# Stick-breaking attention: the sums over later keys from two fp32r parts of the softplus instead of one fp32 tile

## The chip, the cores and the metric

The kernel runs on one core of one Trainium2 chip. The metric is the device time of one execution in microseconds (us), as a median over runs. The profile is of one execution.

## The reference, cut to what matters

The program is a conditioned block (a convolution module and a feed-forward block) and then two blocks with feed-forward layers, one with an RWKV mixer and one with stick-breaking attention, on 256 positions of width 1024. Only the stick-breaking attention is touched: 12 heads of 64, computed for each pair of heads on its own.

```python
z = einsum('bhtd,bhsd->bhts', q, k) * scale
before = s_pos < t_pos
log_keep = where(before, -softplus(z), 0.0)
later = cumsum(log_keep, axis=3, reverse=True) - log_keep
att = where(before, exp(log_sigmoid(z) + later), 0.0)
out = einsum('bhts,bhsd->bhtd', att, v)
```

`later` is a sum over all keys after s. As log_sigmoid(z) = z - softplus(z), the exponent is z minus a sum of softplus over the keys from s on, and a matrix product with a triangle of -1 gives that sum.

## The kernel before, in words

All weights stream through SBUF. Each 128x1024 piece is split by `Stream` into a high fp32r part (ScalarE, L226) and a low one (VectorE, L235), and each product of the large layers is three fp32r matmuls of 256 columns (L377, L378, L372, and L448, L450, L452 for the values). The activations are split in the same way by `split_act` (L625 on ScalarE, L626 on VectorE). Small products of the mixers are plain fp32 matmuls: the profile shows two records for each of them, "x2" where it shows one for an fp32r matmul.

In `StickBreaking`, keys lie on partitions and queries on columns. A head has a z tile of 384 columns in PSUM: 256 queries for the first 128 keys, and 128 queries for the last 128. For a pair p of heads `attention` goes through these steps:

- `scores`: two fp32 matmuls for each head into z (L2294, L2295), then Abs and Exp on ScalarE into e (L2298, L2299);
- `log_keep`: Ln on ScalarE (L2305), max and add on VectorE (L2306), which makes the softplus in e, and the triangular mask on GpSimd (L2308);
- `attend`: three fp32 matmuls for each head add minus the sums to z (L2316 with 256 columns, L2317 and L2319 with 128), then VectorE (L2320) and Exp on ScalarE (L2322);
- `values`: e times V (L2332, L2334), a copy (L2336) and later `split_act` by `operand`.

The steps of pair p - 1 lie between those of pair p: scores p, attend p - 1, log_keep p, values p - 1.

The order of all instructions is written out by `weave`, a planner that runs when the program is built; each engine then works strictly in that order. `weave` has a clock `now` in planned us of TensorE and a clock `dve` of VectorE (it starts at 12.0), and a list of tasks: the attention (priority 1), two tasks of the attention to the memory (3), the projections as `main` (5), and after `main` has ended `products` (5), the first products with the output weights. Each step of a task yields its cost on TensorE, on VectorE, and a further delay. The next task that is due takes a step, by priority; after a step with TensorE cost of another task, `main` comes first. Where no task is due, `idle` writes dummy matmuls of 256 columns (L1455) until one is:

```python
                    self.now += pe
                    t[1] = self.now + more
                    turn = pe > 0 and t[2] is not main
                    if dve:
                        self.dve = max(self.dve, self.now + 0.2) + dve
                        if t[2] is not main:
                            t[1] = self.dve + more + 0.1
...
                later = [t[1] for t in self.tasks if t[1] > self.now]
                self.idle(min(later) - self.now)
                self.now = min(later)
...
        n = int(us / 0.11)
```

`t[1]` is when the task is due again. The costs of `main` are 1.42 for each of the first eight steps, 2.6 (VectorE 1.1) for half a block of values, and 0.66 for each quarter of a projection (VectorE 1.1 at the first quarter of the four). A memory task takes the steps (0.86, 0.7, 0), (0, 0, 1.5), (0, 0.7, 0.3), (0.86, 0, 2.0), (0.86, 0, 1.0) twice. `products` costs 0.66 a step, 16 steps in all, and starts when both memory tasks are done and `n_att` is 5 (`while len(self.mem_out) < 2 or self.n_att < NP - 1: yield`), that is when attend 4 has been issued; its four accumulators take the PSUM banks of the attention. The rest of the output product, the layer norm and the last feed-forward block follow.

At the start `project` fetches the constants of this stage (`sbc`, by a DMA on ScalarE's queue, L2184), loads a table (L342), fills `negones` on GpSimd (L2188), and copies two queries (L2196); the first projections follow.

Of the kernel before, what the change touches and what calls it, by code (L numbers as in the profile page):

```python
# [8 lines left out]
F32 = mybir.dt.float32  # L9
F32R = mybir.dt.float32r  # L10
AF = mybir.ActivationFunctionType
# [4 lines left out]
P = 128  # L16
# [1302 lines left out]
class Norm:  # L1319
# [13 lines left out]
    def sum(self, k0, k1, eng):  # L1333

        b, q = self.b, self.q
        for k in range(k0, k1):
            t = b.ys[:, k]
            self.n += 1
            if eng is None or self.n > KD - self.late:
                self.rest.append(t)  # L1340
            elif eng not in self.sums:
                self.sums[eng] = (t, None)
            else:
                prev, out = self.sums[eng]
                if out is None:
                    out = b.tmp.tile([P, 2, T], F32, name="nsum", tag=f"nsum{len(self.sums)}", bufs=1)
                e = b.nc.vector if eng == "dve" else b.nc.gpsimd
                e.tensor_tensor(out=out[:, q:2, :], in0=prev[:, q:2, :], in1=t[:, q:2, :], op=ALU.add)  # L1348
                self.sums[eng] = (out, out)
# [805 lines left out]
class StickBreaking(Mixer):  # L2155
# [25 lines left out]
    def project(self):  # L2181
        nc, b, mp = self.nc, self.b, self.mp
        sbc = mp.tile([P, 640], F32, name="sbc")
        nc.scalar.dma_start(out=sbc, in_=b.dr["consts_sb"])  # L2184
        b.exp_and_log()
        self.sbk = {n: sbc[:, COFF[n][0]:sum(COFF[n])] for n, _ in CONSTS_SB}
        self.negones = mp.tile([P, P], F32, name="negones")
        nc.gpsimd.memset(self.negones, -1.0)  # L2188
        ys = b.ys.rearrange("p k a t -> p (k a) t")
        self.V = ys[:, 0:6].rearrange("p (a f) t -> p a (f t)", a=2)  # L2190
        self.os = ys[:, 6:12]
        self.mq = ys[:, 14:16]
        self.qk, self.n_val = {}, 0
        pre, b.pre = b.pre, None
        for i in range(2):
            nc.scalar.copy(out=self.mq[:, i, :], in_=pre[2 + i])  # L2196
        self.qk[0] = pre[:2]
        self.add(self.attention(), 1)
        for tl in range(2):
            self.add(self.mem_attention(tl, ys[:, 12 + tl]), SB_MEM)  # L2200
        early = [b.gu_tile() for _ in range(2)]
        yield from b.gemm_outs_parts(early, b.xx)
        for n in range(2):
            self.queries(n + 1, [early[n][:, i, :] for i in range(2)])
        self.mem_go = True
        for kind, i in SB_ORDER[2:]:
            if kind == "p":
                yield from self.pair(i)
                continue
            gu = b.gu_tile()  # L2210
            for u in range(2):
                list(b.gemm_tok(gu, b.xx, u))
                if u:
                    nc.scalar.copy(out=self.V[:, :, i * T:i * T + T], in_=gu)
                    self.n_val += 1
                yield 2.6, 1.1, 0.0
# [41 lines left out]
    def attention(self):  # L2258

        yield 0.0, 0.0, 7.0  # L2260
        self.n_att = 0
        prev = None
        for p in range(NP + 1):
            cur = None
            if p < NP:
                wait = p not in self.qk
                while p not in self.qk:
                    yield
                if wait:
                    yield 0.0, 0.0, 1.0  # L2270
                cur = [self.scores(h, *self.qk[p]) for h in range(2)]
                yield 1.3, 0.9, 0.0
            if prev:
                for z, e in prev:
                    self.attend(z, e)
                self.n_att = p
                yield 1.7, 0.9, 0.0
            if cur:
                for z, e in cur:
                    self.log_keep(z, e)  # L2280
                yield 0.0, 0.9, 0.0
            if prev:
                while self.n_val <= (p - 1) // 2:
                    yield
                yield from self.values(p - 1, prev)
            prev = cur
# [21 lines left out]
        nc.gpsimd.tensor_tensor(out=d, in0=d,  # L2308
                                in1=self.sbk["tri"].unsqueeze(1).to_broadcast([P, 2, P]), op=ALU.mult)

    def attend(self, z, e):

        nc = self.nc
        mm = nc.tensor.matmul
        nt = self.sbk["negtri"]
        mm(z[:, 0:256], lhsT=nt, rhs=e[:, 0:256], start=False, stop=True, skip_group_check=True)  # L2316
        mm(z[:, 128:256], lhsT=self.negones, rhs=e[:, 256:384], start=False, stop=True,  # L2317
           skip_group_check=True)
        mm(z[:, 256:384], lhsT=nt, rhs=e[:, 256:384], start=False, stop=True, skip_group_check=True)  # L2319
        nc.vector.scalar_tensor_tensor(out=e, in0=z, scalar=0.0, in1=self.sbk["bias"], op0=ALU.min,  # L2320
                                       op1=ALU.add)
        nc.scalar.activation(out=e, in_=e, func=AF.Exp)  # L2322
# [38 lines left out]
```

## Time and profile before

| what | value |
|---|---|
| median of 3 runs | 1480.18 us (1478.29 to 1483.04) |
| the profiled execution's own time | 1478.92 us |
| its span, first to last instruction | 1477.1 us |
| granted TensorE clock, mean | 0.976 |
| busy: TensorE, VectorE, ScalarE, GpSimd | 96%, 73%, 58%, 8% |

The projections and the attention of this stage lie from about 1162 to 1262 us of the span. A row of the timeline gives start and duration in us, engine, line, operation, operands and a count; a matmul's duration holds its way through the array, so that the pace of a run of matmuls is read from their starts, not from their durations.

### The profile page before, as it was taken

Reading aid. Unit: us, or ns where it says so; the run is one execution under the profiler, and the core shown is the slowest. Engines: PE = TensorE matmul, PEld = TensorE weight load, DVE = VectorE, ACT = ScalarE, POOL = GpSimd, SP = SyncE. Lnnn points to the kernel's source line nnn. Section 1 sums busy time; section 2 is a strip of 40 time slices with the busy share of each in tenths; the row PEclk is TensorE's granted clock in tenths of the full one; section 3 lists DMA queues with packets and bytes.
Section 4 is the critical chain, followed back from the end, with each engine's and each line's share of the span. In section 5 each row is a group of like instructions: output and inputs, shape, how many; then the busy total and the mean of one; then the engine's idle time right before and its main releaser. Section 6 shows DMA issues by size and latency. Waiting matters only on the chain. (4 is left out here: it accounts for less than half of the span.)

```text
span 1477.1 us, 26067 instructions
## 1 busy us (share of the span) xinstructions
PE 1412.8 (96%) x10664; PEld 1268.2 (86%) x10664; DVE 1074.2 (73%) x1698; ACT 853.8 (58%) x1509; POOL 120.2 (8%) x113
## 2 busy tenths in 40 slices
PE   8888899999999999998999999999999999999997
PEld 7868799998788888898798888888888888888886
DVE  8897788885777667897578776687766755787754
ACT  7686566685656535751346555466554666566542
POOL 1210100001000010040010000110001111100011
PEclk9998899999999999998999999999999999999998
DMA  9775445566355554330034555436545332265540
GB/s 377 295 232 191 178 145 198 200 222 218 124 201 191 200 187 149 109 121 3 2 114 171 200 179 192 184 133 226 195 176 199 126 141 86 95 225 194 198 174 29
DMA packets 39145, 250.38 MB, mean 170 GB/s; under 512 B 4337, under 2 KB 4849, under 8 KB 12274
## 3 DMA queue, kind: packets, MB, share of 16 engines
q1 hardware_dynamic: 38594, 247.60, 46.4%
q8 instruction: 84, 1.38, 0.4%
q10 hardware_dynamic: 432, 1.11, 0.2%
q14 instruction: 35, 0.29, 0.1%
HBM read 247.65 MB, written 1.05 MB: 168 GB/s over the span
## 5 line engine op out<-in xcount | busy, mean ns | idle before, releaser
L235 DVE TENSOR_TENSOR wlo<-wraw,whi 128x1024 fp32r<-128x1024 f32 x416 | 514.4, 1250 | 33.8 <-ACT whi L226 33.2
L226 ACT CAST whi<-wraw 128x1024 fp32r<-128x1024 f32 x416 | 426.4, 1045 | 23.8 <-PE acc L378 6.4
L384 PE MATMUL acc<-hx,whi 128*128 128x512 f32 x880 | 310.8, 398 | 0.0
L384 PE MATMUL acc<-xx,whi 128*128 128x512 f32 x816 | 284.1, 390 | 0.0
L372 PE MATMUL gu<-xx,wlo 128*128 128x256 f32 x1008 | 278.3, 281 | 2.8 <-ACT xx L625 1.7
L372 PE MATMUL acc<-xx,wlo 128*128 128x256 f32 x1008 | 279.4, 282 | 0.0
L372 PE MATMUL acc<-hx,wlo 128*128 128x256 f32 x880 | 247.5, 281 | 0.0
L384 PEld LDWEIGHTS acc<-hx,whi 128*128 128x128 f32 x880 | 165.4, 188 | 40.6
L372 PEld LDWEIGHTS gu<-xx,wlo 128*128 128x128 f32 x1008 | 188.6, 188 | 7.0 <-ACT xx L625 2.9
L372 PEld LDWEIGHTS acc<-xx,wlo 128*128 128x128 f32 x1008 | 189.6, 190 | 0.8
L384 PEld LDWEIGHTS acc<-xx,whi 128*128 128x128 f32 x816 | 153.2, 188 | 32.1
L372 PEld LDWEIGHTS acc<-hx,wlo 128*128 128x128 f32 x880 | 166.1, 189 | 0.0
L384 PE MATMUL gu<-xx,whi 128*128 128x512 f32 x432 | 150.9, 390 | 0.0
L377 PE MATMUL gu<-xx,whi 128*128 128x256 f32 x512 | 148.0, 289 | 2.3 <-ACT u L894 2.3
L378 PE MATMUL gu<-xx,whi 128*128 128x256 f32 x512 | 143.1, 279 | 0.0
L1331 ACT ACTIVATE ys<-ys 128x256 f32<-128x256 f32 (+1 forms) x66 | 28.6, 436 | 152.2 <-DVE ys L1249 135.2
L377 PEld LDWEIGHTS gu<-xx,whi 128*128 128x128 f32 x512 | 96.2, 188 | 9.2 <-issue 6.4
L378 PEld LDWEIGHTS gu<-xx,whi 128*128 128x128 f32 x512 | 96.3, 188 | 0.7 <-issue 0.7
L384 PEld LDWEIGHTS gu<-xx,whi 128*128 128x128 f32 x432 | 81.1, 188 | 17.0
L1348 POOL TENSOR_TENSOR nsum<-ys 128x512 f32<-128x512 f32 (+1 forms) x9 | 12.5, 1386 | 900.0 <-PE acc L384 451.8
L858 ACT COPY lows<-acc 128x256 f32<-128x256 f32 x55 | 20.6, 374 | 97.8 <-PE acc L384 97.7
L1247 DVE SCALAR_TENSOR_TENSOR ys<-xr,acc 128x256 f32<-128x256 f32 x32 | 13.5, 422 | 74.8 <-PE acc L384 74.8
(412 smaller groups left out, 2342.0 us busy)
## 6 DMA issues: line engine op xcount, KB each, us to landing
wraw<-in_w SPq DMA_DIRECT2D x208, 1024.0 KB, 4.8
mraw<-in_mod SPq DMA_DIRECT2D x48, 512.0 KB, 5.8
xr<-in_x SPq DMA_DIRECT2D x2, 512.0 KB, 4.3
m<-in_mem SPq DMA_DIRECT2D x1, 1024.0 KB, 8.2
out<-xr SPq DMA_DIRECT2D x3, 256.0 KB, 2.2
cst<-in_consts SPq DMA_DIRECT2D x1, 546.0 KB
lora<-in_lora ACTq DMA_DIRECT2D x1, 384.0 KB, 3.2
lora_g<-in_lora ACTq DMA_DIRECT2D x1, 384.0 KB, 3.8
```

The costliest lines, as they stand in the source:

```text
L226: b.nc.scalar.copy(out=hi, in_=raw)
L235: b.nc.vector.tensor_tensor(out=lo, in0=raw, in1=hi.bitcast(F32), op=ALU.subtract)
L372: self.nc.tensor.matmul(out, lhsT=wl, rhs=x[:, 0, :], start=start, stop=False, skip_group_check=True)
L377: mm(out, lhsT=wh, rhs=x[:, 0, :], start=start, stop=False, skip_group_check=True)
L378: mm(out, lhsT=wh, rhs=x[:, 1, :], start=False, stop=False, skip_group_check=True)
L384: self.nc.tensor.matmul(bank, lhsT=wh, rhs=x, start=False, stop=stop, skip_group_check=True)
L858: nc.scalar.copy(out=lows[:, 1, :], in_=banks[1][:, 1, :])
L1247: self.nc.vector.scalar_tensor_tensor(out=y, in0=self.xr[:, k, :], scalar=2 * ALPHA, in1=ps[:, 1, :], op0=ALU.mult, op1=ALU.add)
L1331: b.nc.scalar.activation(out=b.ys[:, k0:k1, 1, :], in_=y, func=AF.Square)
L1348: e.tensor_tensor(out=out[:, q:2, :], in0=prev[:, q:2, :], in1=t[:, q:2, :], op=ALU.add)
```

## The change

The softplus tile e is no longer the moving operand. `e_parts` splits it into a high and a low fp32r part (`split_act`: a ScalarE copy and a VectorE subtraction of 128x384, for each head), and `attend` runs each of its three products once for each part, as an fp32r matmul. The two stationary matrices (the triangle and all -1) are held as fp32r in `negs`, made on ScalarE from `sbc` at the start of the stage; the memset on GpSimd goes away. The yields of the attention change with it.

```diff
-        self.negones = mp.tile([P, P], F32, name="negones")
-        nc.gpsimd.memset(self.negones, -1.0)
+        self.negs = mp.tile([P, 2, P], F32R, name="negs")
+        nc.scalar.copy(out=self.negs[:, 0, :], in_=self.sbk["negtri"])
+        nc.scalar.activation(out=self.negs[:, 1, :], in_=self.sbk["negtri"], func=AF.Copy, scale=0.0,
+                             bias=-1.0)
...
             if prev:
-                for z, e in prev:
-                    self.attend(z, e)
+                parts = [self.e_parts(e) for _, e in prev]
+                yield 0.0, 1.1, 0.0
+                for (z, e), x in zip(prev, parts):
+                    self.attend(z, e, x)
                 self.n_att = p
-                yield 1.7, 0.9, 0.0
+                yield 0.9, 0.9, 0.0
...
+    def e_parts(self, e):
+        x = self.mp.tile([P, 2, 384], F32R, name="ep", bufs=2)
+        self.b.split_act(x[:, 0, :], x[:, 1, :], e)
+        return x
+
-    def attend(self, z, e):
+    def attend(self, z, e, x):
...
-        nt = self.sbk["negtri"]
-        mm(z[:, 0:256], lhsT=nt, rhs=e[:, 0:256], start=False, stop=True, skip_group_check=True)
-        mm(z[:, 128:256], lhsT=self.negones, rhs=e[:, 256:384], start=False, stop=True,
-           skip_group_check=True)
-        mm(z[:, 256:384], lhsT=nt, rhs=e[:, 256:384], start=False, stop=True, skip_group_check=True)
+        for i, (w, out, c) in enumerate(((0, z[:, 0:256], slice(0, 256)), (1, z[:, 128:256], slice(256, 384)),
+                                         (0, z[:, 256:384], slice(256, 384)))):
+            for q in range(2):
+                mm(out, lhsT=self.negs[:, w, :], rhs=x[:, q, c], start=False, stop=True,
+                   skip_group_check=True)
```

## Rows read from the trace of the kernel before

**Rows 1.** The page, busy us of TensorE over the span.
```profile
PE 1412.8 (96%) x10664; PEld 1268.2 (86%) x10664; DVE 1074.2 (73%) x1698; ACT 853.8 (58%) x1509; POOL 120.2 (8%) x113
```

**Rows 2.** Windows: stretch, length, busy us and count by engine, PEclk, DMA.
```profile
1205.00:1215.00 10.00, 10.00 (x78) 8.81 (x76) 7.16 (x14) 6.81 (x16) 1.49 (x2) 1.00 0.15 55
1245.00:1255.00 10.00, 9.99 (x80) 8.81 (x79) 7.02 (x9) 6.37 (x13) 2.41 (x2) 1.00 0.30 107
1255.00:1265.00 10.00, 10.00 (x87) 10.00 (x86) 3.46 (x5) 5.31 (x7) 0.00 (x0) 1.00 0.30 107
```

**Rows 3.** Timeline of TensorE, 1217.8 to 1219.8 us: attend for one pair.
```profile
1217.78 0.59 PE L2316 MATMUL z<-e,sbc 128*128 128x256 f32 x2
1218.21 0.38 PE L2317 MATMUL z<-e,negones 128*128 128x128 f32 x2
1218.43 0.39 PE L2319 MATMUL z<-e,sbc 128*128 128x128 f32 x2
1218.66 0.60 PE L2316 MATMUL z<-e,sbc 128*128 128x256 f32 x2
1219.45 0.36 PE L377 MATMUL gu<-xx,whi 128*128 128x256 f32 x1
1219.66 0.28 PE L378 MATMUL gu<-xx,whi 128*128 128x256 f32 x1
```

**Rows 4.** Timeline of TensorE: four transposes of 128 columns and what follows.
```profile
1213.73 0.60 PE L1526 MATMUL r<-head,mex 128*128 128x128 f32 x4
1214.09 0.37 PE L377 MATMUL gu<-xx,whi 128*128 128x256 f32 x1
```

**Rows 5.** Timeline of ScalarE at the start of the stage.
```profile
1170.39 0.33 ACTq L2184 DMA_DIRECT2D sbc<-in_consts_sb  x1
1171.51 1.28 ACT L342 ACT_TABLE_LOAD   x1
1172.80 0.71 ACT L2196 COPY ys<-pre 128x256 f32<-128x256 f32 x2
1173.42 2.00 ACT L226 CAST whi<-wraw 128x1024 fp32r<-128x1024 f32 x2
1177.45 0.36 ACT L2232 COPY k<-gu 128x256 f32<-128x256 f32 x1
```

**Rows 6.** The tile sbc: time of its DMA from issue to landing.
```profile
DMA to landing us min/median/max: 2.8/2.8/2.8
```

**Rows 7.** Timeline of TensorE: the first matmul after the early projections; its idle time.
```profile
1177.87 0.39 PE L448 MATMUL gu<-whi,xx 128*128 128x256 f32 x1 [2.80 <-ACT k L2232]
```

**Rows 8.** Windows: granted clock shortly after that idle time, columns as before.
```profile
1178.90:1182.20 3.30, 3.30 (x18) 3.30 (x16) 2.86 (x4) 3.30 (x6) 0.00 (x0) 0.50 0.56 164
```

**Rows 9.** Timeline of TensorE where the projections have ended: dummies and scores 5.
```profile
1238.51 0.66 PE L1526 MATMUL gu<-head,mex 128*128 128x128 f32 x4
1238.92 0.60 PE L1455 MATMUL gu<-whi 128*128 128x256 f32 x3
1239.44 0.71 PE L2294 MATMUL z<-q,k 64*128 64x256 f32 x4
1240.30 0.50 PE L1455 MATMUL gu<-whi 128*128 128x256 f32 x2
```

**Rows 10.** Groups by shape, 1165 to 1262 us: busy us, mean ns of one, idle before.
```profile
L2299 ACT ACTIVATE e<-e 128x384 f32<-128x384 f32 x12 | 6.3, 524 | 0.4
L626 DVE TENSOR_TENSOR ox<-ys,ox 128x256 fp32r<-128x256 f32 x8 | 3.9, 489 | 9.6 <-ACT ox L625 9.6
L625 ACT CAST ox<-ys 128x256 fp32r<-128x256 f32 x8 | 3.1, 406 | 0.0
L579 DVE TENSOR_TENSOR xx<-xr,xx 128x512 fp32r<-128x512 f32 x3 | 2.1, 693 | 2.3 <-POOL xr L574 2.3
```

**Rows 11.** Timeline of ScalarE after scores 5: first Abs and last Exp.
```profile
1240.40 0.49 ACT L2298 ACTIVATE e<-z 128x384 f32<-128x384 f32 x1 [0.25 <-PE z L2295]
1241.85 0.52 ACT L2299 ACTIVATE e<-e 128x384 f32<-128x384 f32 x1
```

## The prediction, put on record before the change was run

> **What bounds the kernel now.** I read the page first: TensorE is busy 96% of the span [rows 1], so a stage is worth what TensorE issues in it, unless it waits. Then the windows over the stage: in the three stretches shown TensorE is busy 10.00 of 10.00 us, 9.99 and 10.00, while VectorE has 7.2 and ScalarE 6.8 in the fullest of them [rows 2]. So from about 1182 us on, the stage takes as long as the sum of what stands in TensorE's order, and a dummy matmul counts as much as a real one. The timeline shows the one exception, the start: the first matmul of the values stands still for 2.80 us until ScalarE has copied the keys [rows 7]. There ScalarE is the bound: its rows follow one another without a gap from the table load on [rows 5]. Last I read the place where the projections have run out: TensorE goes on with dummies of L1455, three of them and then two [rows 9].
>
> **The change, part by part. The matmuls of attend.** From the first L2316 of a pair to the second head's is 1218.66 - 1217.78 = 0.88 us: 0.43 for 256 columns, 0.22 and 0.23 for the two products of 128 columns [rows 3]. With the next fp32r matmul, which takes 0.21 before its successor starts, where others need 0.12, the pair occupies 1219.66 - 1217.78 - 0.12 = 1.76 us.
>
> After, every product is two fp32r matmuls. Those of 256 columns have a row: 87 of them fill 10.00 us, 0.115 each [rows 2], and I take 0.117, as a cut stretch counts one at either end. An fp32r matmul of 128 columns is nowhere in the trace. From below: half the pace of the 256-column one, 0.058. From above: the pace of a plain fp32 product of 128 columns, 0.22 [rows 3]. Two rows lie between: the four transposes of 128 columns, 1214.09 - 1213.73 = 0.36 us or 0.09 each [rows 4], and the single record of a plain fp32 product, 0.22 / 2 = 0.11, which also loads 128 fp32 weight columns before every pass [rows 3]. I take 0.11, since that load stays. A head is then 2 x 0.117 + 4 x 0.11 = 0.67, a pair 1.35, and six pairs give 6 x (1.76 - 1.35) = 2.5 us. At 0.058 they would give 6 x (1.76 - 0.93) = 5.0; at 0.22 a pair takes 2.23 and they lose 2.8.
>
> The Trainium skill ("TensorE: Matmul & The Clock Gate", section "Back-to-back issue gap") gives some 81 ns for a matmul of 128 columns in a stream of weight loads and matmuls; the transposes' 0.09 is near it. By that figure the six pairs would give an estimated 3.8 us instead of 2.5. The same page (section "LDWEIGHTS") prices a load at its columns over 1.2 GHz, 107 ns for 128, which would speak for 0.11.
>
> **The start.** The two builds of `negs` stand in ScalarE's order behind the table load, and read `sbc`. The DMA is issued at 1170.39 and lands after 2.8 us, at 1173.2 [rows 5, 6]; ScalarE is free at 1171.51 + 1.28 = 1172.8. It waits 0.4 us (0.7 if the landing is counted from the end of the issue). The builds are 128x128; 128x384 takes 0.52 and 128x256 0.41 [rows 10], so about 0.28 each and, overlapped as the rows of L2196 are (0.71 for two), 0.5 for both. Behind them queue the copies of the queries, two weight casts, Abs, Exp, and the key copy that TensorE waits for, with no gap to hide in: 0.9 us (0.8 to 1.4), and the idle time of 2.80 becomes about 3.7. After the idle time the clock goes to 0.50, 1.2 GHz, for the stretch from 1178.9 to 1182.2 [rows 8]; a longer idle time may move or lengthen that stretch, which costs at most as much again as it does now, half of 3.3 us, so up to 1.7. I count none, as it already drops. The memset that goes away ran on GpSimd and nobody waited for it: nothing.
>
> **The parts.** Twelve ScalarE copies of 128x384 at some 0.43 pace (0.52 long) are 5.2 us; twelve subtractions at 0.55, between 0.49 and 0.69 [rows 10], 6.6 us. In 65 us VectorE and ScalarE have a quarter to a third free [rows 2], so this is covered where TensorE has other work. Without cover, the chain shows in the tail. After scores 5, Abs starts at 1240.40 and the last Exp ends at 1242.37 [rows 11]; the high parts would follow (0.9) and the low part of the first head ends about 1243.4, 4.0 us after the scores began at 1239.44 [rows 9].
>
> **The order, which is the large part.** The new yield (0, 1.1, 0) makes the attention due again only 0.2 + 1.1 + 0.1 = 1.4 planned us later, once more for every pair, and attend now advances the clock by 0.9 instead of 1.7. I stepped `weave` through by its rule. With the old yields `main` ends at now = 69.9, and then come pauses of 0.44 (3 dummies), 0.26 (2) and 0.08 (none): the three and two that the trace shows, around scores 5 [rows 9]. With the new ones the attention gets its turns later: when `main` ends, at 64.06, only attend 0 to 2 and values 0 to 2 are issued, where before attend 0 to 3 and values 0 to 3 were, and scores 4 was done too. A whole pair more is left for the time when there is nothing to put between. `products` can't fill it, since it waits for attend 4. What follows is: 0.44 pause, scores 4, 1.2, parts 3, 1.4, attend 3, 1.2, log_keep 4, 1.2, values 3, 1.3, scores 5, 1.2, parts 4, 1.4, attend 4. Each pause is 0.2 + the step's VectorE cost + its delay + 0.1 (scores, attend and log_keep 1.2, values 1.3). At 0.11 each, rounded down, that makes 3 + 10 + 12 + 10 + 10 + 11 + 10 + 12 = 78 dummies where there were 5. After attend 4 `products` covers the rest, as before. The real work is the same sum in another order, with as many changes between fp32 and fp32r, so the dummies come on top: 73 x 0.117 = 8.5 us.
>
> Twice the dummies are a little too few: before attend 3 and attend 4, TensorE has scores (0.88 and a change of 0.2) and 22 dummies (2.57), 3.65 us, against the 4.0 of the parts' chain: 0.35 each, 0.7 in all (0 to 1.5). Elsewhere two or three quarters of a projection lie between parts and attend.
>
> **The sum.** Against the profiled execution's 1478.9: + 8.5 + 0.9 + 0.7 - 2.5 = + 7.6, so 1486.5. That execution lay 1.3 under the median of the runs shown, so a median of runs becomes 1487.8, and I say 1488 (0.5% slower).
>
> **Rivals.**
> The 128-column fp32r matmuls run at the pace of plain fp32 (0.22): then each product of 128 columns costs twice what it did. For it: no row has fp32r with so few columns, and the kernel uses at least 256 everywhere else. Against it: nothing but the transposes, which are another operation. The sum is 8.5 + 0.9 + 0.7 + 2.8 = + 12.9, 1493.
>
> The saving is at its full size: 0.058 for 128 columns and a start of 0.8, no stalls. 8.5 + 0.8 - 5.0 = + 4.3, 1484.5, at the edge of what can be told.
>
> Not slower: the dummies do not come. The place is the stretch between the last values block and the first product with the output weights; the mechanism, that the attention keeps up with `main` and leaves no pair over. Then 0.9 + 0.7 - 2.5 = - 0.9, 1479.3, no change; with 0.058 for 128 columns, 0.8 - 5.0 = - 4.2, 1476. It decides when fewer than 45 of the 73 dummies come: 45 x 0.117 = 5.3, which with - 0.9 is the 4.4 us of 0.3%. Against it: the stepping gives the trace's own order for before, down to three and two.
>
> **Chances.** The forecast 0.60, the plain fp32 pace 0.22, the full saving 0.10, no dummies 0.08. Faster or slower than 0.3% (4.4 us), about what a measurement of this kernel can tell from no change: the no-dummies case goes mostly to "same", with 0.02 to faster; of the full saving two thirds are "same"; of the forecast little is. So faster 0.02, same 0.14, slower 0.84. The range: from the full saving less a us of spread between runs, 1483.5, to the plain fp32 pace, 1493, plus 1 for a longer stretch at 1.2 GHz or stalls, 1494. The forecast's own range is 1485.5 to 1490.
>
> **What would show it.** L1455 with 78 matmuls in this stage instead of 5, in blocks of some 22, 20, 11 and 22 (some records may be missing). L2317 and L2319's successors at 0.11 between starts (0.22 in the first rival, 0.06 to 0.09 in the second). The first L448 idle for about 3.7 us, still released by the key copy. A pair of attends in 1.35 us without the slow fp32r matmul behind it. Idle time of TensorE before attend 3 and 4 of a few tenths, on VectorE's low part. It would be wrong if the dummies were few, or if the parts were late in the middle of the stage, where I count no wait: then TensorE would stand before attend 0 to 2 behind ScalarE's queue.

## The result, and the profile after

The changed kernel is slower: 1488.77 us median (1487.48 to 1489.33, 4 runs) against 1479.24 us for the kernel before, a ratio of 1.0062 with a 95% interval of 1.0049 to 1.0074. 1488.0 was predicted, between 1483.5 and 1494.0. The profiled execution has a span of 1487.2 us against 1477.1.

The page's line of engine counts goes beside [rows 1]. It shows 73 more matmuls, and as many more weight loads, on a TensorE that is as busy as before.

```profile
PE 1422.0 (96%) x10737; PEld 1280.7 (86%) x10737; DVE 1078.8 (73%) x1710; ACT 861.0 (58%) x1523; POOL 119.5 (8%) x112
```

These are the groups by shape from 1165 to 1275 us, with busy us, mean ns of one and the idle time before it: the dummies (L1455), the 72 matmuls of attend (L2328) on the tile of the parts (`ep`), and the two halves of the split (L625 and L626).

```profile
L1455 PE MATMUL gu<-whi 128*128 128x256 f32 x78 | 10.6, 288 | 0.0
...
L2328 PE MATMUL z<-ep,negs 128*128 128x128 f32 x48 | 6.7, 262 | 0.0
...
L626 DVE TENSOR_TENSOR ep<-e,ep 128x384 fp32r<-128x384 f32 x12 | 6.2, 554 | 9.3 <-ACT ep L625 9.3
L2328 PE MATMUL z<-ep,negs 128*128 128x256 f32 x24 | 6.1, 314 | 0.5 <-DVE ep L626 0.4
L625 ACT CAST ep<-e 128x384 fp32r<-128x384 f32 x12 | 5.6, 511 | 0.0
```

TensorE's timeline from the last memory step to the first products with the output weights, the answer to [rows 9]:

```profile
1236.79 0.62 PE L1455 MATMUL gu<-whi 128*128 128x256 f32 x3
1237.34 0.71 PE L2299 MATMUL z<-q,k 64*128 64x256 f32 x4
1237.87 0.39 PE L2300 MATMUL z<-q,k 64*128 64x128 f32 x4
1238.20 2.89 PE L1455 MATMUL gu<-whi 128*128 128x256 f32 x22
1241.04 0.38 PE L2328 MATMUL z<-ep,negs 128*128 128x256 f32 x1
1241.63 1.46 PE L2328 MATMUL z<-ep,negs 128*128 128x256 f32 x11 [0.21 <-DVE ep L626]
1242.93 2.60 PE L1455 MATMUL gu<-whi 128*128 128x256 f32 x20
1245.46 0.66 PE L2342 MATMUL gu<-e,ys 128*64 128x256 f32 x4
1245.94 0.40 PE L2344 MATMUL gu<-e,ys 128*64 128x128 f32 x4
1246.26 1.57 PE L1455 MATMUL gu<-whi 128*128 128x256 f32 x11
1247.76 0.71 PE L2299 MATMUL z<-q,k 64*128 64x256 f32 x4
1248.30 0.40 PE L2300 MATMUL z<-q,k 64*128 64x128 f32 x4
1248.62 2.89 PE L1455 MATMUL gu<-whi 128*128 128x256 f32 x22
1251.35 1.86 PE L2328 MATMUL z<-ep,negs 128*128 128x256 f32 x12
1253.05 0.33 PE L377 MATMUL acc<-ox,whi 128*128 128x256 f32 x1
```

The rows show a whole pair of heads, and the front half of another, with nothing but dummies between their steps: 3, 22, 20, 11 and 22, in the places that the stepping of the planner gave. From the start of each block to the next row they fill 0.55 + 2.84 + 2.53 + 1.50 + 2.73 = 10.15 us, where the five of before fill 0.52 + 0.44 = 0.96 [rows 9]. That is 9.2 us more, the changes between fp32 and fp32r around the blocks included. It is not yet the price of the order: with the yields alone (e1_yields_only, below) the stage is 1278.42 - 1170.20 = 108.22 us long, from the issue of the constants' DMA to the first matmul of the next norm (L1383), against 100.05 before, so 8.2 us longer. The other rows of TensorE, added up from start to start, are 0.9 us shorter there. 0.4 of that are the last two pairs of attends, at 1.67 us instead of 1.78 and 1.95.

A pair of attends in the middle of the stage, the answer to [rows 3], and the pair before it:

```profile
1225.62 1.48 PE L2328 MATMUL z<-ep,negs 128*128 128x256 f32 x12
1226.94 0.33 PE L377 MATMUL gu<-xx,whi 128*128 128x256 f32 x1
1227.11 0.28 PE L378 MATMUL gu<-xx,whi 128*128 128x256 f32 x1
```

```profile
1209.14 0.28 PE L2328 MATMUL z<-ep,negs 128*128 128x256 f32 x1
1209.62 1.47 PE L2328 MATMUL z<-ep,negs 128*128 128x256 f32 x11 [0.20 <-DVE ep L626]
1210.92 0.33 PE L377 MATMUL gu<-xx,whi 128*128 128x256 f32 x1
```

Twelve matmuls take 1226.94 - 1225.62 = 1.32 us; less four of 256 columns at 0.117 that leaves 0.106 for each of the eight of 128 columns. The pair occupies 1227.11 - 1225.62 - 0.12 = 1.37 us where it occupied 1.76, because the next matmul still takes 0.05 longer than usual; with that counted in, a matmul of 128 columns costs 0.113.

This pair doesn't wait. The one before it does: its second matmul starts 0.48 us after the first, where 0.12 is usual, since the low part is late. The profile counts only 0.20 of that as idle, from the modelled end of the first. From its first start to the next row the six pairs take 1.39, 1.78, 1.32, 1.89, 1.70 and 1.31 us. Against 1.31 each that is 1.5 us of waits in all: 0.97 in the tail and 0.56 ahead of it. (1.31 is what the six pairs take in e5_last_yield, where nothing waits for the parts, 1.41 the one behind an fp32 step.)

The start: ScalarE's timeline, and TensorE's first matmul after the early projections (the answers to [rows 5] and [rows 7]).

```profile
1172.25 1.28 ACT L342 ACT_TABLE_LOAD   x1
1173.95 0.30 ACT L2189 CAST negs<-sbc 128x128 fp32r<-128x128 f32 x1 [0.42 <-DMA sbc<-in_consts_sb]
1174.15 0.31 ACT L2190 ACTIVATE negs<-sbc 128x128 fp32r<-128x128 f32 x1
1174.37 0.70 ACT L2199 COPY ys<-pre 128x256 f32<-128x256 f32 x2
```

```profile
1179.42 0.58 PE L448 MATMUL gu<-whi,xx 128*128 128x256 f32 x1 [3.58 <-ACT k L2235]
```

ScalarE waits 0.42 us for the DMA and then builds the matrices in 0.42, and TensorE's idle time grows from 2.80 to 3.58.

The sum is 8.2 for the order + 0.8 for the start - 6 x 0.39 for the matmuls + 1.5 for the waits = + 8.2. From the issue of the constants' DMA to the first L1383 it is 1270.44 - 1170.39 = 100.05 us before and 1279.26 - 1171.14 = 108.12 after, + 8.1. The other 2.0 us of the span lie outside. The DMA is issued 0.75 later; in the seven experiments, with nothing changed ahead of it, it is issued between 1168.7 and 1171.4. And 1.2 come after the stage, where the granted clock is lower. Two windows, of 10 us from that first L1383, of the kernel before and of the changed kernel (the third number from the end is the granted clock):

```profile
1270.44:1280.44 10.00, 8.73 (x55) 7.59 (x54) 7.54 (x18) 3.58 (x7) 0.36 (x1) 0.83 0.28 105
```

```profile
1279.26:1289.26 10.00, 8.85 (x48) 8.36 (x47) 6.32 (x15) 3.29 (x7) 0.38 (x1) 0.66 0.31 106
```

0.66 instead of 0.83 is 3.4 us more at half the rate, which is at most 1.7 us of work. Nothing was changed there. In the nine kernels' traces that window has 0.66 five times, with 207.0 to 208.1 us from its start to the end, and 0.83 four times, with 206.7 to 207.2. So the 1.2 us fit the lower clock; why it differs is not shown.

### The profile page after: what moved, and what is told of

Its sections match the earlier page's. It is cut to its first block, busy times and chain, and to the rows that moved or that the text cites. A ratio compares the mean times of both kernels' runs of the same rounds, so it can differ in the third digit from the quotient of the medians.

```text
span 1487.2 us, 26244 instructions
## 1 busy us (share of the span) xinstructions
PE 1422.0 (96%) x10737; PEld 1280.7 (86%) x10737; DVE 1078.8 (73%) x1710; ACT 861.0 (58%) x1523; POOL 119.5 (8%) x112
```

## The experiments

The theory was: the new yields change the planner's order, a pair of heads is left without other work beside it, and that costs the time; fp32r itself gains 2.3 us and the start costs 0.8. The rival: the splits cost the time, as 24 more instructions on ScalarE and VectorE and waits for them, and the dummies stand where TensorE would have waited. Ratios are to the kernel before, with 95% intervals.

**The yields alone** (e1_yields_only), on the kernel before:

```diff
             if prev:
+                yield 0.0, 1.1, 0.0
                 for z, e in prev:
                     self.attend(z, e)
...
-                yield 1.7, 0.9, 0.0
+                yield 0.9, 0.9, 0.0
```

> The kernel before, with plain fp32 in attend and no parts, but with the changed kernel's three yields. The order theory (the slowdown is the dummies that the planner adds): 78 dummies in the stage instead of 5, 73 x 0.117 = 8.5 us more, 1479.2 + 8.5 = 1487.7, a ratio of 1.0058. The rival (the slowdown comes from the work of splitting, 24 more instructions on ScalarE and VectorE and their waits, and the dummies only fill waits): no parts, so no change, 1479.2.

Measured 1487.6 us, 1.0063 (1.0050 to 1.0076): as slow as the whole change, without a single split or fp32r matmul in attend. The one line on the dummies (count, durations, first and last start) of this kernel:

```profile
L1455 PEld LDWEIGHTS gu<-whi x78: 186/192/193, 1235.8 to 1249.8; 128*128 128x128 f32 x78
```

TensorE waits for nothing new in this stage, so the 73 dummies stand in no wait's place. The rival falls as the cause of the slowdown. The stage is 8.2 us longer than before, as in the result above.

**Which of the two yields** (e7_attend_yield): the kernel before with attend's cost alone changed.

```diff
-                yield 1.7, 0.9, 0.0
+                yield 0.9, 0.9, 0.0
```

> The kernel before, fp32 and without parts, with attend yielding 0.9 instead of 1.7 and no other change. It tells the two changed yields apart: stepping the planner with this one alone gives 5 dummies (3 and 2) again, with the extra yield alone 68 or more. So no change, 1479.2 within 0.2%. If the lower cost of attend were what lets the projections run out early, it would be slower by 5 us or more.

Measured 1479.66, 1.0002 (0.9993 to 1.0011), with 5 dummies. The lower cost does nothing by itself. With the run before it that leaves the extra yield, by itself or together with the lower cost; it was not run alone.

**The old order with the parts where the change puts them** (e2_old_order), on the changed kernel:

```diff
                 parts = [self.e_parts(e) for _, e in prev]
-                yield 0.0, 1.1, 0.0
                 for (z, e), x in zip(prev, parts):
...
-                yield 0.9, 0.9, 0.0
+                yield 1.7, 0.9, 0.0
```

> The changed kernel with the order of the kernel before: no yield between the parts and attend, and attend yields 1.7 again. Order theory: 5 dummies; start + 0.8, matmuls - 2.3; and now TensorE stands before attend for the parts, since the split needs about 4.0 us from the start of the scores and attend stood 2.3 to 3.8 us behind them in the kernel before: 1.7, 1.6, 1.2, 0.5 and 0.2 us for five pairs, 5.2 in all. Sum 1479.2 + 0.8 - 2.3 + 5.2 = 1482.9, ratio 1.0025. The rival (splitting work as such): it stays at 1488.

Measured 1496.88, 1.0128 (1.0115 to 1.0141): the slowest of all, with 5 dummies, far above either figure. Its waits of TensorE in the stage (us in total, times, longest), and two windows of it:

```profile
PE z L2327 <- ACT ep L625: 9.4, 6, 2.5
...
PE z L2327 <- DVE ep L626: 1.5, 5, 0.7
```

```profile
1189.00:1192.00 3.00, 1.53 (x8) 1.03 (x8) 1.56 (x4) 2.63 (x7) 0.00 (x0) 0.85 0.12 49
1192.00:1198.00 6.00, 6.00 (x29) 6.00 (x30) 3.10 (x9) 3.42 (x9) 0.38 (x1) 0.50 0.00 0
```

The wait for the parts is 10.9 us, twice the 5.2 that I had reckoned, because ScalarE's queue often has more before the parts than Abs and Exp. Before one attend its timeline reads:

```profile
1208.21 0.53 ACT L2303 ACTIVATE e<-e 128x384 f32<-128x384 f32 x1
1208.64 1.03 ACT L226 CAST whi<-wraw 128x1024 fp32r<-128x1024 f32 x1
1209.79 0.59 ACT L2217 COPY ys<-gu 128x512 f32<-128x512 f32 x1
1210.28 0.93 ACT L625 CAST ep<-e 128x384 fp32r<-128x384 f32 x2
```

A weight cast and a copy of values stand in between. The waits bring a second price: behind three of the six pairs the granted clock falls to 0.50, that is 1.2 GHz. The stage takes 1287.24 - 1169.12 = 118.1 us, 18.1 more than before; 10.9 + 0.8 - 2.3 leaves 8.7. The windows of 10 us put 6.8 of them to the lower clock: they have 0.87 and 0.96 from 1170 on, 0.66 from 1190, 0.83 from 1240 and from 1260, and 1.00 else, where the kernel before has 0.94 and 0.89 from 1170 on and 1.00 else. The other 1.9 fit what the profile leaves out of a wait, as in the pair of the result above. Behind one of the longest waits the clock didn't fall:

```profile
1225.93 0.38 PE L2327 MATMUL z<-ep,negs 128*128 128x256 f32 x1 [2.45 <-ACT ep L625]
```

```profile
1230.00:1240.00 10.00, 8.68 (x60) 6.55 (x58) 4.07 (x7) 6.21 (x17) 2.41 (x2) 1.00 0.28 105
```

So the extra yield had a purpose: it gives the split time. It is the place of the parts that makes it needed.

**The old order with the parts ahead of the next scores** (e3_parts_first), on the run before it:

```diff
+                if prev:
+                    parts = [self.e_parts(e) for _, e in prev]
                 cur = [self.scores(h, *self.qk[p]) for h in range(2)]
                 yield 1.3, 0.9, 0.0
+            elif prev:
+                parts = [self.e_parts(e) for _, e in prev]
             if prev:
-                parts = [self.e_parts(e) for _, e in prev]
                 for (z, e), x in zip(prev, parts):
```

> As the run before it in this list (old order, 5 dummies), but the parts of the last pair are issued ahead of the scores of the next, so that ScalarE makes them before Abs and Exp. Order theory: no dummies more and no wait for the parts, 1479.2 + 0.8 - 2.3 = 1477.7, ratio 0.999. The rival (splitting work as such loads ScalarE and VectorE and holds up the weight splits): still slower than before, 1484 to 1488.

Measured 1479.88, 1.0009 (1.0000 to 1.0019). All splits are done, and the slowdown is gone: the stage takes 99.99 us, as before. The time is 2.2 us above the 1477.7 that I expected, as two waits of TensorE remain, both before the last attend, whose e comes from GpSimd just before:

```profile
PE z L2330 <- DVE ep L626: 0.7, 1, 0.7
...
PE z L2330 <- ACT ep L625: 0.5, 1, 0.5
```

**The last pair** (e5_last_yield), where products with the output weights are ready to go between:

```diff
             elif prev:
                 parts = [self.e_parts(e) for _, e in prev]
+                yield 0.0, 1.1, 0.0
```

> Old order, parts ahead of the scores (as in e3_parts_first), and for the last pair alone, which has no scores beside it but has products of the output weights to put between, the new yield between parts and attend. In e3_parts_first TensorE stood 0.52 and 0.65 us before the last attend. Order theory: 5 dummies, that wait goes, start + 0.8 and matmuls - 2.3: 1479.2 - 1.5 = 1477.7, ratio 0.999. Rival (the splits cost something of their own on ScalarE and VectorE): it stays at e3_parts_first's 1.0009 or above.

Measured 1477.26, 0.9993 (0.9984 to 1.0002). The two waits are gone from the trace, and the dummies stay at 5. The step from e3_parts_first is 0.0016, or 2.6 us by the medians, more than the 1.2 us that the profile counts as idle, but by the intervals alone it isn't certain. In the traces the stage is 99.99 - 98.18 = 1.8 us shorter. 1.7 of that is the last pair: from the row before it to the row behind it, it takes 3.14 us with the waits and 1.43 without.

**The start** (e6_late_builds), the builds behind the first query and key copies:

```diff
-        nc.scalar.copy(out=self.negs[:, 0, :], in_=self.sbk["negtri"])
-        nc.scalar.activation(out=self.negs[:, 1, :], in_=self.sbk["negtri"], func=AF.Copy, scale=0.0,
-                             bias=-1.0)
...
         self.mem_go = True
+        nc.scalar.copy(out=self.negs[:, 0, :], in_=self.sbk["negtri"])
+        nc.scalar.activation(out=self.negs[:, 1, :], in_=self.sbk["negtri"], func=AF.Copy, scale=0.0,
+                             bias=-1.0)
```

> As e5_last_yield, with the two builds of the fp32r matrices moved behind the first query and key copies on ScalarE, where the constants have long landed. The first values matmul should stand still for 2.8 us again instead of 3.6. By the sum, 1479.2 - 2.3 = 1476.9, ratio 0.9985, if the start is worth its 0.8 us; equal to e5_last_yield if the start is hidden after all.

Measured 1477.27, 0.9987 (0.9977 to 0.9997). The first values matmul, in e5_last_yield and in this kernel:

```profile
1178.73 0.58 PE L448 MATMUL gu<-whi,xx 128*128 128x256 f32 x1 [3.61 <-ACT k L2235]
```

```profile
1178.18 0.39 PE L448 MATMUL gu<-whi,xx 128*128 128x256 f32 x1 [2.79 <-ACT k L2235]
```

The trace shows the 0.8 us of the start come and go with the builds, and the stage is 98.18 - 97.45 = 0.7 us shorter; the times of the two kernels can't tell it, as their intervals overlap. This version beats both kernels, by 0.13% against the one before (0.03% to 0.23%). In the traces its stage is 100.05 - 97.45 = 2.6 us shorter than before: fp32r's gain of some 2.3 us and the slower last pairs of before, with nothing paid for them.

**The changed order without its dummies** (e4_no_dummies), on the changed kernel:

```diff
+    def idle(self, us):
+        pass
```

> The changed kernel with its order, but the planner's pauses in this stage write no dummy matmuls. If the dummies as such were the price, all 78 x 0.117 = 9.1 us come back: 1479.6. By my theory the price is the pair that has nothing beside it: TensorE then waits about 2.9 us twice for the parts and 1.35 for the weights of values, and nothing for scores 5, 7.1 us in place of 9.1 of dummies and 0.6 of waits, so 1488.8 - 2.6 = 1486.2; a lower granted clock after a long wait could take some of that.

Measured 1489.84, 1.0077 (1.0064 to 1.0090): nothing came back, neither all the dummies (1479.6) nor the 2.6 us that I expected. Its waits, and windows over the tail:

```profile
PE z L2331 <- ACT ep L625: 5.2, 2, 2.8
...
PE z L2331 <- DVE ep L626: 0.6, 3, 0.2
```

```profile
1236.00:1241.00 5.00, 2.24 (x19) 1.48 (x15) 1.04 (x3) 4.15 (x11) 0.00 (x0) 1.00 0.61 210
1241.00:1246.00 5.00, 4.79 (x18) 3.69 (x19) 2.32 (x5) 2.05 (x5) 0.00 (x0) 0.52 0.00 0
1246.00:1251.00 5.00, 2.54 (x12) 1.60 (x10) 1.33 (x4) 3.39 (x8) 1.41 (x2) 0.80 0.00 0
1251.00:1256.00 5.00, 4.79 (x23) 4.66 (x23) 3.01 (x5) 2.11 (x5) 0.00 (x0) 0.54 0.00 0
```

TensorE waits 2.76 and 2.46 us for the parts instead of working on dummies, and the stretch behind each wait runs at 0.52 and 0.54. The changed kernel, with its dummies, has 1.00 in the same place:

```profile
1240.00:1250.00 10.00, 9.79 (x80) 8.72 (x79) 4.00 (x8) 5.30 (x13) 1.42 (x2) 1.00 0.01 2
```

In windows of 10 us the clock without dummies is 0.99 and 0.84 from 1170 on, 0.66 in both from 1240 to 1260, and 1.00 else; the changed kernel has 0.96 and 0.87 from 1170 on and 1.00 else. That is 6.8 us more of lost work. The waits are 5.8 us where the changed kernel has 0.4. 108.1 - 10.15 + 5.4 + 6.8 = 110.2, and the stage takes 1281.96 - 1171.27 = 110.7. So the dummies as such aren't the price; the uncovered pair is, and it is paid in dummies, or in waits and a lower clock.

**All stages side by side.** The stage from the issue of the constants' DMA to the first L1383, in the one profiled execution of each kernel, leaves out what varies ahead of it and behind it:

| kernel | stage, us | against before |
|---|---|---|
| before | 100.05 | |
| changed | 108.12 | + 8.1 |
| e1_yields_only | 108.22 | + 8.2 |
| e7_attend_yield | 100.08 | 0.0 |
| e2_old_order | 118.12 | + 18.1 |
| e3_parts_first | 99.99 | - 0.1 |
| e5_last_yield | 98.18 | - 1.9 |
| e6_late_builds | 97.45 | - 2.6 |
| e4_no_dummies | 110.69 | + 10.6 |

## Why the prediction was right

**The order** was the cause, and was put at 8.5 us. The yields alone make the stage 8.2 us longer. All 78 dummies came, in the blocks that the stepping gave; the run of the yields alone (as slow) and that of the old order with the parts ahead (e3_parts_first, as fast as before) hold the step up from both sides. The sum held the rest of the work to be the same on both sides. It wasn't quite: the changes between fp32 and fp32r around the blocks make the dummies 9.2 us instead of 8.5, and the other rows are 0.9 shorter. These two slips nearly cancel. What the prediction didn't see is that the dummies could not simply have been left out.

**The matmuls of attend** were put at 0.11 us for 128 columns, and take 0.106 (0.113 with the slower matmul behind them). A pair that doesn't wait went from 1.76 to 1.37 (predicted 1.35), 2.3 us in all instead of 2.5, ahead of the waits. The rivals at 0.22 and at 0.058 are both out. That the load of the fp32 weights sets the pace is argued, not tested by a run; for it speak that half the columns take nearly the time of all, and the starts of the loads, twelve in 1226.88 - 1225.51 = 1.37 us or 0.114 each:

```profile
1225.51 1.45 PEld L2328 LDWEIGHTS z<-ep,negs 128*128 128x128 f32 x12
1226.88 0.19 PEld L377 LDWEIGHTS gu<-xx,whi 128*128 128x128 f32 x1
```

The Trainium skill ("TensorE: Matmul & The Clock Gate", section "LDWEIGHTS") prices a load at its columns over 1.2 GHz, which is 107 ns for 128, and the trace is near it; its 81 ns for a matmul of 128 columns in a stream ("Back-to-back issue gap") is too low for these.

**The start** was put at 0.9 us: 0.4 for the DMA and 0.5 for the builds. It is 0.42 and 0.42, and the idle time grew by 0.78. The clock fell behind it before and after, and for as long: 0.94 and 0.89 in the windows of 10 us from 1170 on before, 0.96 and 0.87 after, 1.7 us of lost work both times.

**The waits for the parts** were put at 0.7 us in the tail (0 to 1.5), and none elsewhere. They are 1.5: 0.97 at attend 3 and 4, and 0.56 at attend 0 and 1. So one of the signs of being wrong that the prediction names, parts late in the middle of the stage, did show, at a small size: this term was half of what it should have been. That it stayed small has a reason that is narrower than the text: the planner's pause of 1.4 and 22 dummies covered the split nearly exactly. My figure of 4.0 us for the chain of the parts holds where ScalarE has nothing else queued (at attend 4, whose second matmul starts at 1251.75, it is 1251.75 - 1247.76 = 3.99); in the run with the old order it had, and the wait came to twice the one reckoned.

**The time itself** was met more closely than the sum. The sum gave + 7.6 us, and the stage is 8.1 longer. The medians differ by 9.5, as 2.0 us in the profiled execution lie outside the stage, in terms that the sum doesn't have. That 1488 came within 0.8 us of the median is in part luck: it started from a median of three runs, 1480.18, that lies 0.9 above the median with one run more.

**No dummies**, the rival on the other side, is what e3_parts_first and e6_late_builds make true: 1.0009 and 0.9987, where that rival had 1479.3 and, with a saving at its largest, 1476.

## What to carry to other kernels

Where a planner writes out the order, its costs are part of the change: step it through with the new numbers before pricing the instructions, and look at the end of the covering work, where a step that came late leaves a chain with nothing beside it. An operand that needs a split or a cast is best prepared one step earlier, ahead of the next work in the same queue, rather than paid for with a delay in the plan. Half the columns for each fp32r matmul was not half the time here: 0.106 us with 128 columns, 0.117 with 256.

## What the runs showed of the hardware that was not expected

The granted clock fell to 0.50, 1.2 GHz, after TensorE had waited 2.76 us, and to about as much after 2.46 us (e4_no_dummies), with fp32r and fp32 matmuls before and between, and it cost about as much as the waits: 6.8 us beside the 5.8 that the profile counts as idle. With dummy matmuls in the same place it stayed at 1.00. The length of a wait alone doesn't tell: in e2_old_order the clock fell behind waits of 1.46 and 2.31 us, and stayed at 1.00 behind 2.45 and 1.54.

An fp32r matmul of 128 columns with a new weight load keeps a pace of 0.106 us (0.113 with the slower matmul behind the pair), against 0.117 for 256 columns: half the columns for nine tenths of the time or more.
